# Hybrid attention block on one core: the modulation's vector steps moved to other stages, with their own load queue

## Chip, core and metric

The kernel runs on 1 core of one Trainium2 chip. The metric is device microseconds of one execution. Three runs of the kernel before took 1920.5, 1924.43 and 1924.89 us; their median is 1924.43 us.

The engines are named as in the profile: PE is TensorE (matmul; PEld its weight loads), DVE is VectorE, ACT is ScalarE, POOL is GpSimd and SP is SyncE. SP only issues DMAs here; POOL issues some DMAs and computes a little.

## What is computed

Two layers over 256 latent and 256 context tokens (512 columns in all, kept transposed as `xT`, 1024 features in 8 tiles of 128), in fp32 accuracy.

```python
for layer in range(2):
    mod_x = (silu(c) @ ada_w[layer] + ada_b[layer])        # 9 rows of 1024: shift, scale, gate x 3
    mod_c = (silu(c_ctx) @ ada_w[layer] + ada_b[layer])
    x   = ffn_branch(x, mod_x, 0, ...)     # h + 0.5*gate * swiglu(rms(h)*(1+scale) + shift), d_ff 2816
    ctx = ffn_branch(ctx, mod_c, 0, ...)
    x, ctx = mixer(...)                    # neighbourhood attention, spatial gating, retention; gate row 5
    x   = ffn_branch(x, mod_x, 6, ...)
    ctx = ffn_branch(ctx, mod_c, 6, ...)   # not in the last layer
return x
```

The modulation is a product of a vector with a 1024 x 9216 matrix per layer, once for the latent and once for the context stream ("two streams"). Of layer 1, context needs rows 0 to 4 only.

## The kernel before

**Products.** Each fp32 weight chunk `wr` [128 x up to 1024] is split into a rounded part `wh` (ACT, L89) and the rest `wl` (DVE, L100), and a product is three matmuls (L206 to L208). `Stream` (L64) walks one list of all weight chunks: SP loads into 3 raw buffers, and 4 buffers each hold `wh` and `wl`. `take()` keeps the splits up to three chunks ahead, so the split of an output's next weights stands, on ACT and DVE, ahead of this output's own end.

**FFN.** `ffn(l, f)` runs in two halves of 11 hidden tiles j: up products `g` and `u`, the gate, and then the down products `d` of 8 outputs m with 11 tiles each (`down`, 33 matmuls). After each m DVE adds the result to `xT` (`residual`, L441); in the second half ACT then squares `xT` and DVE sums the squares (`acc`, L341) for the next norm. The last two m of a second half are done one stream at a time (half width), and the statistics (`ss`, L350 on PE, `pow` on POOL at L355) of the latent stream follow while PE does the context's.

FFNs (0, 1) and (1, 0), "direct" in `DIRECT`, do 4 tiles j of the first half plainly and the other 18 by a Winograd scheme (`Seven`) with seven products instead of eight. It needs sums of the normed input, `th` and `tl` [128, 4, 4, 256] each (`sums`: DVE adds, ACT rounds to `th`, DVE subtracts to `tl`), and combined weights `q` and `r`, made by accumulating DMAs from POOL (L529, L530) and a POOL add (L558). After the last tile j of the second half `th` and `tl` are not read again. FFN (1, 1), "one", has the latent stream only.

**Modulation steps.** All of it but two rows of layer 0 is done by DVE: a block `aw` (128 outputs x 1024 inputs, 512 KB) is loaded, and a step (L290, `tensor_tensor_reduce` with the broadcast vector `cb`) gives the 128 values for one stream; a block serves one or two steps. After 8 blocks `fin` adds the bias (L295) and makes the factors (L299, L303). `ada_steps(l, count)` makes the list of these steps for the next blocks of layer l; in front of each step it issues the load of the block that is as many blocks ahead as there are buffers.

**Order.** Code order is engine order (`manual_schedule`). Every product calls `pump`, which adds `pace[0]` (times the product's width over 512) to a credit and takes one item of the list `bg` for each whole credit. So steps stand between products at an even pace, on DVE's one queue, and their loads on SP's one queue, among the weights' loads. A step whose block has not landed holds up all that stands behind it on DVE, and a load whose buffer is not free all that stands behind it on SP.

Before, the 112 steps of layer 1 are divided so: 26 beside FFN (0, 0) after layer 0's 112 (pace 0.34, 5 buffers), 18 beside the first half's and 25 beside the second half's down products of FFNs (0, 1) and (1, 0) each, with 2 buffers that the Winograd `q` shares (tag "aw").

Of the kernel before, what the change touches and what calls it, by code (L numbers as in the profile page):

```python
# [9 lines left out]
F32 = mybir.dt.float32  # L10
F32R = mybir.dt.float32r
# [26 lines left out]

DIRECT = {(0, 1): (4, 0), (1, 0): (4, 0)}

ADA_DOWN = {(0, 1): (18, 25), (1, 0): (18, 25)}

STAT, OS, FS, SPR = 3, 3.5, 2, 12

# [9 lines left out]
SUMS = 1.0  # L54
GPACE = (0.4, 0.55)
OPACE = (0.8, 0.8)
APACE = 0.34
NPACE = (0.95, 1.0)
RPACE = (1.2, 1.4)

# [74 lines left out]
def tile_hybrid_dit(ctx: ExitStack, tc: tile.TileContext, t_x, t_c, t_cb, t_ada0, t_ada, t_adab, t_nw, t_w1, t_w2,  # L135
# [83 lines left out]
    with tc.manual_schedule():  # L219
# [36 lines left out]
        mod = [const.tile([128, 72, 2], F32, name=f"mod{l}") for l in range(L)]  # L256
        amul = [const.tile([128, 3, KT, 2], F32, name=f"amul{l}") for l in range(L)]

        adap = [None, 0]
        cb = const.tile([128, 2, D], F32, name="cb")  # L260

        ada_todo = [[(r, b) for r in range(2 if l == 0 else 0, 9) for b in range(KT)] for l in range(L)]
# [1 line left out]
        def ada_steps(l, count):  # L264

            def streams(r):

                return 1 if l == L - 1 and r > 4 else 2  # L270

            todo = []
            while ada_todo[l] and sum(streams(r) for r, b in todo) < count:
                todo.append(ada_todo[l].pop(0))
            tiles = {}
            nload = [0]

            def loads(n):
                while nload[0] < min(n, len(todo)):
                    r, b = todo[nload[0]]  # L280
                    t = tiles[r, b] = adap[0].tile([128, CHUNK], F32, tag="aw", name="aw", bufs=adap[1])
                    SP.dma_start(out=t, in_=t_ada[l, r, b])
                    nload[0] += 1

            def step(i, s, n):
                loads(i + adap[1])
                r, b = todo[i]
                t = tiles[r, b]
                junk = adap[0].tile([128, CHUNK], F32, tag="cu", name="junk", bufs=1) if s < n - 1 else t
                V.tensor_tensor_reduce(out=junk, in0=t, in1=cb[:, s], scale=1.0, scalar=0.0, op0=ALU.mult, op1=ALU.add,  # L290
                                       accum_out=mod[l][:, 8 * r + b, s:s + 1])

            def fin(r, n):
                mo = mod[l][:, 8 * r:8 * r + 8, 0:n]
                V.tensor_tensor(out=mo, in0=mo, in1=adab[:, l, 8 * r:8 * r + 8].unsqueeze(2).to_broadcast([128, KT, n]),  # L295
                                op=ALU.add)
                i, k = divmod(r, 3)
                if k == 1:
                    V.scalar_tensor_tensor(out=amul[l][:, i, :, 0:n], in0=mo, scalar=1.0,  # L299
                                           in1=nw[:, l, i, :].unsqueeze(2).to_broadcast([128, KT, n]),  # L300
                                           op0=ALU.add, op1=ALU.mult)
                elif k == 2 and i != 1:
                    V.tensor_scalar(out=mo, in0=mo, scalar1=0.5, scalar2=None, op0=ALU.mult)  # L303

            out = [lambda: loads(adap[1])]
            for i, (r, b) in enumerate(todo):
                n = streams(r)
                out += [lambda i=i, s=s, n=n: step(i, s, n) for s in range(n)]
                if b == KT - 1:
                    out.append(lambda r=r, n=n: fin(r, n))  # L310
            return out
# [148 lines left out]
        class Seven:  # L460
# [7 lines left out]

            def __init__(self, pool, gated, l, f):
                self.pool, self.gated, self.l, self.f = pool, gated, l, f  # L470
                self.th = pool.tile([128, 4, 4, T], F32R, name="th")
                self.tl = pool.tile([128, 4, 4, T], F32R, name="tl")
                self.raw, self.part = {}, {}

            def sums(self, q):

                x = []

                def work():
                    t = self.pool.tile([128, CHUNK], F32, tag="cu", name="sum", bufs=1)  # L480
                    u = self.pool.tile([128, NT], F32, tag="ur", name="sum", bufs=1)
                    x.extend(v.rearrange("p (k t) -> p k t", k=2) for v in (t[:, 0:NT], t[:, NT:2 * NT], u))

                a, b = slice(0, T), slice(T, NT)
                k0, k1 = slice(2 * q, 2 * q + 2), slice(4 + 2 * q, 6 + 2 * q)

                def whole(n, k, c):
                    V.tensor_tensor(out=x[n], in0=hTh[:, k, c].bitcast(F32), in1=hTl[:, k, c].bitcast(F32), op=ALU.add)

                def high(i, n, sign=1.0):  # L490
                    S.activation(out=self.th[:, i, k0], in_=x[n], func=AF.Copy, scale=sign)

                def low(i, n, sign=1.0):
                    V.scalar_tensor_tensor(out=self.tl[:, i, k0], in0=x[n], scalar=sign,
                                           in1=self.th[:, i, k0].bitcast(F32), op0=ALU.mult, op1=ALU.subtract)

                def comb(n, p, r, op):
                    V.tensor_tensor(out=x[n], in0=x[p], in1=x[r], op=op)

                def normed(f):  # L500
                    f.when = lambda: all(kt in feeds[self.l, 2 * self.f, n].done for kt in range(KT) for n in range(2))
                    return f

                sub = ALU.subtract
                return [normed(lambda: (work(), whole(0, k0, b))), lambda: whole(1, k0, a),
                        lambda: (comb(1, 1, 0, sub), high(0, 1)), lambda: whole(2, k1, b),
                        lambda: low(0, 1), lambda: (comb(0, 2, 0, sub), high(2, 0)),
                        lambda: (comb(2, 2, 1, ALU.add), high(1, 2, -1.0)), lambda: low(2, 0),
                        lambda: whole(0, k1, a), lambda: low(1, 2, -1.0),
                        lambda: (comb(0, 2, 0, sub), high(3, 0)), lambda: low(3, 0)]  # L510

            def load(self, j):
                if j >= 2 * JH:
# [112 lines left out]
        def ffn(l, f, lead, norms, steps=None, tail=None):  # L626
# [7 lines left out]
            with ExitStack() as es:  # L634
# [8 lines left out]
                def seven_pool():  # L643
                    nonlocal seven
                    pool = es.enter_context(tc.tile_pool(name="seven", bufs=1))
                    seven = Seven(pool, fp, l, f)
                    adap[:] = pool, 2

                if (l, f) in DIRECT:
                    seven_pool()  # L650
                elif not one:
                    adap[:] = fp, ADA_BUFS
                for half in range(2):
                    aTh = fp.tile([128, JH, NT], F32R, tag="aTh", name="aTh")
                    aTl = fp.tile([128, JH, NT], F32R, tag="aTl", name="aTl")
# [116 lines left out]
                                    kt == 0, kt == JH - 1)  # L772

                    split_tail = half == 1 and len(streams) == 2
                    if seven:
                        bg.extend(ada_steps(1, ADA_DOWN[l, f][half]))
                        pace[0], pace[1] = len(bg) / (JH * (KT - 1 if half else KT - 3)), 0.0
                    ahead = seven and half == 0
                    for m in range(KT - 2 if split_tail else KT):
                        a, b = 0, T * len(streams)  # L780
                        wa, wb = ws.take(), ws.take(AHEAD - 1)
                        ps = mm_bank("d")
                        if ahead and m == KT - 3:
                            drain_bg()
                            seven.load(JH)
                            seven.load(JH + 1)
                            seven.add(JH)
# [905 lines left out]
        for l in range(L):  # L1693
# [2 lines left out]
            n2 = {s: Norm(l, 2, s) for s in range(1 if last else 2)}  # L1696
            n3 = {} if last else {s: Norm(l + 1, 0, s) for s in range(2)}
            if l == 0:
                bg.extend(ada_steps(0, 112) + ada_steps(1, 26))
                bg.insert(1, small_inputs)  # L1700
                bg.insert(2, lambda: S.activation(out=cb, in_=cb, func=AF.Silu))
                bg.insert(15, prepare)
# [127 lines left out]
```

## Time and profile before

| | us |
|---|---|
| median of the runs | 1924.43 |
| the profiled execution's own time | 1931.78 |
| its span, first to last instruction | 1929.6 |
| PE busy | 1825.9 (95%) |
| DVE busy | 1312.8 (68%) |
| ACT busy | 728.7 (38%) |
| POOL busy | 239.7 (12%) |
| mean granted TensorE clock, share of full | 0.973 |
| time DMA queues' packets took: SP's, POOL's (share of 16 engines) | 42.7%, 6.5% |

Matmuls are pipelined: a busy PE is one with no gap, and one matmul of 512 columns is listed with some 0.39 us while the next starts 0.23 us after it. Idle time is put down to what ended it. The clock column of a window is the mean over it, 1.00 being full speed.

### The profile page before, as it was taken

The numbers are of one execution on the slowest core, as the hardware profiler recorded it, in microseconds if no ns is written. First come the engines' busy times: TensorE is split into PE (matmuls) and PEld (weight loads), VectorE is DVE, ScalarE is ACT, GpSimd is POOL, SyncE is SP. The second block draws the span as 40 slices with busy tenths as digits, with TensorE's granted clock in tenths as the row PEclk, the third lists the DMA queues.
The fourth block names the chain that finished last, engine by engine and source line by source line (L and its number), as shares of the span: only waits on it lengthen the run. The fifth ranks groups of instructions, "written<-read, shape, count | busy, mean of one in ns | idle before, by whom it ended". The sixth has DMA issues, their size and how long they took to land. (4 is left out here: it accounts for less than half of the span.)

```text
span 1929.6 us, 29556 instructions
## 1 busy us (share of the span) xinstructions
PE 1825.9 (95%) x11592; PEld 1579.8 (82%) x11592; DVE 1312.8 (68%) x2214; ACT 728.7 (38%) x1211; POOL 239.7 (12%) x261
## 2 busy tenths in 40 slices
PE   7999999999999999999999799979987699999999
PEld 5788888887678898978996689869975576889999
DVE  5789888764445567866886678747865554566665
ACT  3322222244542344522452244314421255444443
POOL 0000000011133201202220013002300012410000
PEclk9999999999998999999999899989997799999999
DMA  7756665333111125646754446466745442335555
GB/s 286 244 194 221 227 221 196 123 124 113 61 55 45 55 88 131 147 159 192 188 139 152 135 120 170 141 200 173 170 150 174 139 142 72 99 121 171 180 186 153
DMA packets 104763, 292.19 MB, mean 151 GB/s; under 512 B 12208, under 2 KB 18992, under 8 KB 104496
## 3 DMA queue, kind: packets, MB, share of 16 engines
q1 hardware_dynamic: 94256, 271.43, 42.7%
q0 software_dynamic: 10368, 18.88, 6.5%
q8 instruction: 91, 1.49, 0.3%
q14 instruction: 48, 0.39, 0.1%
HBM read 289.21 MB, written 1.05 MB: 150 GB/s over the span
## 5 line engine op out<-in xcount | busy, mean ns | idle before, releaser
L100 DVE TENSOR_TENSOR wl<-wr,wh 128x1024 fp32r<-128x1024 f32 (+2 forms) x304 | 322.1, 1086 | 109.4 <-ACT wh L89 108.6
L89 ACT CAST wh<-wr 128x1024 fp32r<-128x1024 f32 (+2 forms) x304 | 275.6, 932 | 207.4 <-DMA wr<-in_w_dram 97.8
L206 PE MATMUL d<-aTh,wh 128*128 128x512 f32 (+1 forms) x770 | 281.8, 366 | 43.1 <-ACT wh L89 43.1
L208 PE MATMUL d<-aTh,wl 128*128 128x512 f32 (+1 forms) x770 | 281.1, 365 | 20.1 <-DVE wl L100 20.0
L207 PE MATMUL d<-aTl,wh 128*128 128x512 f32 (+1 forms) x770 | 279.1, 362 | 0.2 <-DVE aTl L680 0.2
L206 PEld LDWEIGHTS d<-aTh,wh 128*128 128x128 f32 x770 | 154.3, 200 | 68.0 <-ACT wh L89 46.9
L290 DVE CUSTOM_DVE_ANT_0 aw<-aw,cb 128x1024 f32<-128x1024 f32 x128 | 156.6, 1223 | 65.4 <-DMA aw<-in_ada_dram 62.5
L208 PEld LDWEIGHTS d<-aTh,wl 128*128 128x128 f32 x770 | 153.5, 199 | 49.1 <-DVE wl L100 27.5
L207 PEld LDWEIGHTS d<-aTl,wh 128*128 128x128 f32 x770 | 153.9, 200 | 22.2 <-DVE aTl L680 0.5
L206 PE MATMUL g<-hTh,wh 128*128 128x512 f32 (+2 forms) x448 | 152.9, 341 | 4.4 <-ACT wh L89 3.4
L207 PE MATMUL g<-hTl,wh 128*128 128x512 f32 (+2 forms) x448 | 151.5, 338 | 1.3 <-DVE hTl L366 1.1
L208 PE MATMUL g<-hTh,wl 128*128 128x512 f32 (+2 forms) x448 | 151.5, 338 | 0.6 <-DVE wl L100 0.5
L208 PE MATMUL u<-hTh,wl 128*128 128x512 f32 (+2 forms) x448 | 150.6, 336 | 0.5 <-DVE wl L100 0.5
L206 PE MATMUL u<-hTh,wh 128*128 128x512 f32 (+2 forms) x448 | 150.3, 336 | 0.0
L207 PE MATMUL u<-hTl,wh 128*128 128x512 f32 (+2 forms) x448 | 150.3, 335 | 0.0
L290 DVE CUSTOM_DVE_ANT_0 junk<-aw,cb 128x1024 f32<-128x1024 f32 x96 | 117.1, 1220 | 41.1 <-DMA aw<-in_ada_dram 40.6
L214 PE MATMUL nat<-wh,hTh 128*128 128x512 f32 (+2 forms) x384 | 138.3, 360 | 0.0
L216 PE MATMUL nat<-wh,hTl 128*128 128x512 f32 (+2 forms) x384 | 128.5, 335 | 0.4 <-DVE hTl L366 0.4
L215 PE MATMUL nat<-wl,hTh 128*128 128x512 f32 (+2 forms) x384 | 128.4, 334 | 0.0
L583 PE MATMUL p<-hTh,wl 128*128 128x256 f32 x432 | 124.1, 287 | 1.6 <-DVE wl L552 0.5
L583 PE MATMUL p<-th,wl 128*128 128x256 f32 x432 | 122.0, 282 | 0.2 <-DVE wl L552 0.2
L582 PE MATMUL p<-hTl,wh 128*128 128x256 f32 x432 | 121.4, 281 | 0.0
(261 smaller groups left out, 4106.6 us busy)
## 6 DMA issues: line engine op xcount, KB each, us to landing
aw<-in_ada_dram SPq DMA_DIRECT2D x144, 512.0 KB, 5.0
wr<-in_w_dram SPq DMA_DIRECT2D x140, 512.0 KB, 4.4
wr<-in_wi_dram SPq DMA_DIRECT2D x56, 512.0 KB, 3.6
wr<-in_w_dram SPq DMA_DIRECT2D x64, 384.0 KB, 3.6
wr<-in_w_dram SPq DMA_DIRECT2D x64, 320.0 KB, 2.9
q<-in_w_dram SPq DMA_DIRECT2D x72, 256.0 KB, 3.3
q<-in_w_dram POOLq DMA_DIRECT2D x72, 256.0 KB, 5.6
ur<-in_w_dram SPq DMA_DIRECT2D x36, 256.0 KB, 4.4
```

What stands on the lines that cost most here:

```text
L89: self.nc.scalar.copy(out=h[:, :n], in_=self.raw[i][:, :n])
L100: self.nc.vector.tensor_tensor(out=lo[:, :n], in0=t[:, :n], in1=h[:, :n].bitcast(F32), op=ALU.subtract)
L206: PE.matmul(out=ps, lhsT=wh[:, col:col + 128], rhs=hh[rhs_sl], start=start, stop=False)
L207: PE.matmul(out=ps, lhsT=wh[:, col:col + 128], rhs=hl[rhs_sl], start=False, stop=False)
L208: PE.matmul(out=ps, lhsT=wl[:, col:col + 128], rhs=hh[rhs_sl], start=False, stop=stop)
L214: PE.matmul(out=ps, lhsT=hh[lhs_sl], rhs=wh[:, wc], start=start, stop=False)
L215: PE.matmul(out=ps, lhsT=hh[lhs_sl], rhs=wl[:, wc], start=False, stop=False)
L216: PE.matmul(out=ps, lhsT=hl[lhs_sl], rhs=wh[:, wc], start=False, stop=stop)
L290: V.tensor_tensor_reduce(out=junk, in0=t, in1=cb[:, s], scale=1.0, scalar=0.0, op0=ALU.mult, op1=ALU.add, accum_out=mod[l][:, 8 * r + b, s ...
L582: PE.matmul(out=ps, lhsT=wh[:, cw], rhs=tl, start=False, stop=False)
L583: PE.matmul(out=ps, lhsT=wl[:, cw], rhs=th, start=False, stop=n == 3)
```

## The change

Four things change. The steps of layer 1 are divided anew (`ADA1`): 48 beside FFN (0, 0) at pace 0.355, none beside the first halves of (0, 1) and (1, 0), 27 and 29 beside their second halves' down products, 8 beside the up products of the last FFN's first half. The lists take whole blocks, so 28, 29 and 7 steps stand there; they need 14, 27 and 7 loads. In the second halves the four buffers are quarters of a tile with the tag of `th`, so they lie in its memory, and the loads are issued by POOL. In FFN (1, 1) there are four buffers of its own pool, loaded by SP. In `sums` each cast to `th` stands one item later than the sum that it reads (13 items instead of 12).

```diff
-ADA_DOWN = {(0, 1): (18, 25), (1, 0): (18, 25)}
+ADA1 = {(0, 0): 48, (0, 1): 27, (1, 0): 29, (1, 1): 8}
...
-APACE = 0.34
+APACE = 0.355
...
-        adap = [None, 0]
+        adap = [None, 0, SP, None]
...
                     r, b = todo[nload[0]]
-                    t = tiles[r, b] = adap[0].tile([128, CHUNK], F32, tag="aw", name="aw", bufs=adap[1])
-                    SP.dma_start(out=t, in_=t_ada[l, r, b])
+                    t = tiles[r, b] = adap[0](nload[0])
+                    adap[2].dma_start(out=t, in_=t_ada[l, r, b])
...
-                junk = adap[0].tile([128, CHUNK], F32, tag="cu", name="junk", bufs=1) if s < n - 1 else t
+                junk = adap[3].tile([128, CHUNK], F32, tag="cu", name="junk", bufs=1) if s < n - 1 else t
...
-                self.th = pool.tile([128, 4, 4, T], F32R, name="th")
+                self.th = pool.tile([128, 4, 4, T], F32R, tag="th", name="th")
...
-                return [normed(lambda: (work(), whole(0, k0, b))), lambda: whole(1, k0, a),
-                        lambda: (comb(1, 1, 0, sub), high(0, 1)), lambda: whole(2, k1, b),
-                        lambda: low(0, 1), lambda: (comb(0, 2, 0, sub), high(2, 0)),
...
+                return [normed(lambda: (work(), whole(0, k0, b))), lambda: whole(1, k0, a), lambda: comb(1, 1, 0, sub),
+                        lambda: (whole(2, k1, b), high(0, 1)), lambda: comb(0, 2, 0, sub),
+                        lambda: (low(0, 1), high(2, 0)), lambda: comb(2, 2, 1, ALU.add),
...
                     seven = Seven(pool, fp, l, f)
-                    adap[:] = pool, 2
 
                 if (l, f) in DIRECT:
                     seven_pool()
-                elif not one:
-                    adap[:] = fp, ADA_BUFS
+                else:
+                    nb = ADA_BUFS - one
+                    adap[:] = lambda i: fp.tile([128, CHUNK], F32, tag="aw", name="aw", bufs=nb), nb, SP, fp
+                if one:
+                    bg.extend(ada_steps(1, ADA1[l, f]))
+                    pace[0], pace[1] = len(bg) / (KT * (JH - 1)), 0.0
...
-                    if seven:
-                        bg.extend(ada_steps(1, ADA_DOWN[l, f][half]))
-                        pace[0], pace[1] = len(bg) / (JH * (KT - 1 if half else KT - 3)), 0.0
+                    if one and half == 0:
+                        drain_bg()
+                    if seven and half:
+
+                        aw = seven.pool.tile([128, 4, CHUNK], F32, tag="th", name="aw")
+                        adap[:] = lambda i: aw[:, i % 4], 4, G, seven.pool
+                        bg.extend(ada_steps(1, ADA1[l, f]))
+                        pace[0], pace[1] = len(bg) / (JH * (KT - 1)), 0.0
...
                         if ahead and m == KT - 3:
-                            drain_bg()
                             seven.load(JH)
...
-                bg.extend(ada_steps(0, 112) + ada_steps(1, 26))
+                bg.extend(ada_steps(0, 112) + ada_steps(1, ADA1[0, 0]))
```

How instructions move is seen at three places. The first is DVE at the end of the second half of FFN (0, 0); `d` are the down products, `ss` the statistics of the next norm. Before, from the residual of the last full-width output m = 5 on (the sums of squares, L341, are left out in both):

```order
L441 SCALAR_TENSOR_TENSOR xT_69<-d_3011,mod0_93,xT_69 128x256 x2
L100 TENSOR_TENSOR wl_3055<-wr_2955,wh_3053 128x768
L100 TENSOR_TENSOR wl_3061<-wr_3003,wh_3059 128x640
L441 SCALAR_TENSOR_TENSOR xT_69<-d_3065,mod0_93,xT_69 128x256
L441 SCALAR_TENSOR_TENSOR xT_69<-d_3103,mod0_93,xT_69 128x256
L353 TENSOR_SCALAR v_3158<-ss_3153 128x2
```

Now, from the same residual on (each step's row that reads the accumulator is left out):

```order
L441 SCALAR_TENSOR_TENSOR xT_69<-d_3056,mod0_93,xT_69 128x256 x2
L100 TENSOR_TENSOR wl_3106<-wr_2990,wh_3104 128x768
L100 TENSOR_TENSOR wl_3112<-wr_3048,wh_3110 128x640
L290 ISA junk_3132,mod1_94<-aw_2999,cb_97 128x1024
L290 ISA aw_2999,mod1_94<-aw_2999,cb_97 128x1024
L441 SCALAR_TENSOR_TENSOR xT_69<-d_3116,mod0_93,xT_69 128x256
L290 ISA junk_3173,mod1_94<-aw_3022,cb_97 128x1024
L290 ISA aw_3022,mod1_94<-aw_3022,cb_97 128x1024
L441 SCALAR_TENSOR_TENSOR xT_69<-d_3157,mod0_93,xT_69 128x256
L295 TENSOR_TENSOR mod1_94<-mod1_94,adab_78 128x16
L303 TENSOR_SCALAR mod1_94<-mod1_94 128x16
L353 TENSOR_SCALAR v_3217<-ss_3212 128x2
```

The steps (L290) used to end with the third output; now they go on to the last half-width residual, and `fin` (L295, L303) stands directly in front of the statistics' `v`.

The second place is the queue that issues the blocks `aw` in the second half's down products of FFN (1, 0). Before, it is SP's, and `wr` are the weights of the down products:

```order
L79 DMA wr_13155<-in_w2_dram 128x640 [waits DMAHW1_49,DVE_49]
L79 DMA wr_13161<-in_w2_dram 128x768 [waits DMAHW4_49,DMAHW2_49,DVE_49]
L282 DMA aw_13167<-in_ada_dram 128x1024 [waits DMAHW3_49]
L282 DMA aw_13176<-in_ada_dram 128x1024 [waits DVE_49]
L282 DMA aw_13188<-in_ada_dram 128x1024 [waits DMAHW5_49,DVE_49]
L282 DMA aw_13200<-in_ada_dram 128x1024 [waits DMAHW6_49,DVE_49]
L79 DMA wr_13221<-in_w2_dram 128x640 [waits DMAHW7_49,DVE_49]
L79 DMA wr_13227<-in_w2_dram 128x768 [waits DMAHW1_49,DMAHW0_49,DVE_49]
```

Now it is POOL's, behind the last POOL add of the Winograd weights:

```order
L557 TENSOR_TENSOR wr_12523<-wr_12523,q_12525 128x512 [waits DMASW4_49,DMAHW7_49,DVE_49,Activation_49]
L282 DMA aw_12917<-in_ada_dram 128x1024 [waits PE_49]
L282 DMA aw_12917<-in_ada_dram 128x1024 x3
L282 DMA aw_12917<-in_ada_dram 128x1024 [waits DVE_49]
L282 DMA aw_12917<-in_ada_dram 128x1024 [waits DMASW3_49,DVE_49]
L282 DMA aw_12917<-in_ada_dram 128x1024 [waits DVE_49]
L282 DMA aw_12917<-in_ada_dram 128x1024 [waits DMASW5_49,DVE_49]
```

The loads left SP's queue, where four of them stood between two pairs of weights; on POOL nothing but loads follows until the statistics. The first waits for PE, the last reader of `th`.

The third place is DVE at the start of the second half's down products of FFN (0, 1) now, with the semaphores that each step waits for (accumulator rows left out); `aw` is the one tile with four quarters:

```order
L290 ISA junk_9221,mod1_94<-aw_9191,cb_97 128x1024 [waits DMASW4_49]
L290 ISA aw_9191,mod1_94<-aw_9191,cb_97 128x1024 [waits DVE_49]
L290 ISA junk_9240,mod1_94<-aw_9191,cb_97 128x1024 [waits DMASW5_49]
L441 SCALAR_TENSOR_TENSOR xT_69<-d_9198,mod0_93,xT_69 128x256 [waits PE_49]
L441 SCALAR_TENSOR_TENSOR xT_69<-d_9198,mod0_93,xT_69 128x256
L100 TENSOR_TENSOR wl_9250<-wr_9138,wh_9248 128x768 [waits DMAHW0_49,Activation_49]
L100 TENSOR_TENSOR wl_9256<-wr_9172,wh_9254 128x640 [waits DMAHW1_49,Activation_49]
L290 ISA aw_9191,mod1_94<-aw_9191,cb_97 128x1024 [waits DVE_49]
L290 ISA junk_9278,mod1_94<-aw_9191,cb_97 128x1024 [waits DMASW6_49]
L290 ISA aw_9191,mod1_94<-aw_9191,cb_97 128x1024 [waits DVE_49]
L290 ISA junk_9297,mod1_94<-aw_9191,cb_97 128x1024 [waits DMASW7_49]
```

The first step on each block waits for the next DMA semaphore of POOL's queue in turn (DMASW4, 5, 6, 7), the second step on a block for none.

## Rows read from the trace of the kernel before

**Rows 1.** Windows, down-product stages: span, busy us (instructions) by engine, PEclk, DMA share, GB/s.

```profile
160.40:222.00 61.60, 61.60 (x266) 49.48 (x265) 56.44 (x95) 14.51 (x19) 0.00 (x0) 1.00 0.71 238
344.40:407.40 63.00, 63.00 (x342) 53.83 (x342) 39.20 (x70) 19.02 (x34) 0.69 (x1) 1.00 0.31 99
830.90:899.70 68.80, 64.01 (x267) 50.49 (x266) 41.60 (x69) 13.23 (x18) 4.86 (x5) 0.98 0.62 189
1011.90:1102.60 90.70, 74.72 (x344) 61.74 (x342) 59.53 (x106) 19.11 (x35) 0.72 (x1) 0.87 0.43 142
1224.70:1305.30 80.60, 66.76 (x267) 51.98 (x266) 42.81 (x71) 13.83 (x18) 4.81 (x5) 0.94 0.61 192
1415.80:1532.50 116.70, 78.48 (x343) 64.49 (x342) 57.66 (x104) 19.11 (x35) 0.71 (x1) 0.80 0.48 159
```

**Rows 2.** Waits, 1415.8 to 1532.5: who waited for whom, us, times, longest.

```profile
DVE aw L290 <- DMA aw<-in_ada_dram: 46.7, 12, 6.2
...
PE d L206 <- ACT wh L89: 31.2, 5, 9.7
```

**Rows 3.** Waits, 1224.7 to 1305.3.

```profile
PE d L208 <- DVE wl L100: 13.6, 4, 5.5
```

**Rows 4.** Waits of SP's queue, 1415.8 to 1532.5.

```profile
SPq L282 <- DVE mod L290: 40.5, 15, 7.0
```

**Rows 5.** Timeline of DVE from 1458.5: start, us, operation [idle before <- releaser].

```profile
1458.51 0.87 DVE L441 SCALAR_TENSOR_TENSOR xT<-d,mod,xT 128x256 f32<-128x256 f32 x2
1459.47 0.82 DVE L341 TENSOR_TENSOR acc<-acc,sq 128x256 f32<-128x256 f32 x2
1460.58 1.70 DVE L100 TENSOR_TENSOR wl<-wr,wh 128x768 fp32r<-128x768 f32 x2 [0.30 <-ACT wh L89]
1462.19 1.22 DVE L290 CUSTOM_DVE_ANT_0 aw<-aw,cb 128x1024 f32<-128x1024 f32 x1
...
1468.94 1.23 DVE L290 CUSTOM_DVE_ANT_0 aw<-aw,cb 128x1024 f32<-128x1024 f32 x1 [5.52 <-DMA aw<-in_ada_dram]
...
1473.89 1.23 DVE L290 CUSTOM_DVE_ANT_0 aw<-aw,cb 128x1024 f32<-128x1024 f32 x1 [2.46 <-DMA aw<-in_ada_dram]
...
1475.04 0.87 DVE L441 SCALAR_TENSOR_TENSOR xT<-d,mod,xT 128x256 f32<-128x256 f32 x2
```

**Rows 6.** Timeline of DVE, first step of FFN (0, 1)'s second half.

```profile
1021.68 1.23 DVE L290 CUSTOM_DVE_ANT_0 junk<-aw,cb 128x1024 f32<-128x1024 f32 x1 [4.45 <-DMA aw<-in_ada_dram]
```

**Rows 7.** Timeline, statistics at the end of FFN (0, 1).

```profile
1093.52 0.38 PE L350 MATMUL ss<-ones,sq 128*128 128x1 f32 x2 [3.21 <-ACT sq L337]
```

**Rows 8.** Windows, first 50 us.

```profile
0.00:50.00 50.00, 37.36 (x328) 28.02 (x329) 26.01 (x66) 17.42 (x35) 1.60 (x6) 1.00 0.80 291
```

**Rows 9.** Timeline of POOL, an accumulating DMA's issue.

```profile
785.71 1.19 POOL L530 DMA_DIRECT2D q<-in_w_dram  x1
```

**Rows 10.** Waits of DVE, 60 to 345 (first FFN).

```profile
DVE sg L673 <- PE u L208: 5.6, 7, 1.4
...
DVE xT L441 <- PE d L208: 4.1, 5, 1.5
```

**Rows 11.** Windows, up products of the last FFN's first half.

```profile
1740.00:1805.00 65.00, 65.00 (x541) 65.00 (x540) 43.75 (x68) 32.48 (x47) 0.00 (x0) 1.00 0.50 163
```

**Rows 12.** Waits, 725 to 760 (the sums of FFN (0, 1)).

```profile
ACT th L491 <- DVE sum L498: 14.6, 6, 3.3
...
PE g L206 <- ACT wh L89: 2.3, 1, 2.3
```

**Rows 13.** The page's part 6: DMA issues, count, KB each, us to landing.

```profile
aw<-in_ada_dram SPq DMA_DIRECT2D x144, 512.0 KB, 5.0
...
q<-in_w_dram SPq DMA_DIRECT2D x72, 256.0 KB, 3.3
q<-in_w_dram POOLq DMA_DIRECT2D x72, 256.0 KB, 5.6
```

**Rows 14.** Windows, 750 to 800 (Winograd products).

```profile
750.00:800.00 50.00, 49.95 (x379) 47.80 (x378) 38.98 (x51) 25.04 (x38) 14.96 (x14) 1.00 0.71 175
```

More of the change, by code (lines that the diff above doesn't have):

```diff
@@ L504, in sums @@
                 sub = ALU.subtract
-                return [normed(lambda: (work(), whole(0, k0, b))), lambda: whole(1, k0, a),
-                        lambda: (comb(1, 1, 0, sub), high(0, 1)), lambda: whole(2, k1, b),
-                        lambda: low(0, 1), lambda: (comb(0, 2, 0, sub), high(2, 0)),
-                        lambda: (comb(2, 2, 1, ALU.add), high(1, 2, -1.0)), lambda: low(2, 0),
-                        lambda: whole(0, k1, a), lambda: low(1, 2, -1.0),
-                        lambda: (comb(0, 2, 0, sub), high(3, 0)), lambda: low(3, 0)]
+                return [normed(lambda: (work(), whole(0, k0, b))), lambda: whole(1, k0, a), lambda: comb(1, 1, 0, sub),
+                        lambda: (whole(2, k1, b), high(0, 1)), lambda: comb(0, 2, 0, sub),
+                        lambda: (low(0, 1), high(2, 0)), lambda: comb(2, 2, 1, ALU.add),
+                        lambda: (low(2, 0), high(1, 2, -1.0)), lambda: whole(0, k1, a), lambda: low(1, 2, -1.0),
+                        lambda: comb(0, 2, 0, sub), lambda: high(3, 0), lambda: low(3, 0)]
             def load(self, j):
```

## Prediction

> **What bounds the kernel now.** I first read the busy shares and the clock in the table above: TensorE is busy for 95% of the span and DVE for 68%, so only time in which TensorE waits, or runs below its full clock, can be won. Next I cut the span into the stages of the code. The down products of the first three FFNs have the same shape, 8 outputs m of 11 x 3 matmuls, so the stage without a wait is a ruler: 61.6 us for a first half and 63.0 us for a second half [rows 1]. The reader is to see in the other four windows that the same products take 68.8, 90.7, 80.6 and 116.7 us, with DMA at half its share and the granted clock at 0.80 to 0.98. The excess is 7.2 + 27.7 + 19.0 + 53.7 = 107.6 us: nearly all that TensorE loses in this kernel, and all of it beside the modulation steps with two buffers.
>
> Then the waits. In the worst window DVE stands 46.7 us before steps whose block `aw` has not landed, and TensorE stands 31.2 us for `wh` [rows 2]; in the first half of FFN (1, 0) it stands 13.6 us for `wl` [rows 3]. The queue of SP shows the loop: it stands 40.5 us before an `aw` load until a step frees one of the two buffers, and the weights' loads stand behind it [rows 4]. One turn of DVE closes it [rows 5]: residuals, sums of squares, the two splits of the next weights, a step, then 5.52 us for a load, two steps, 2.46 us for the next. In order, the residual and the splits wait behind the late block; the turn takes 16.5 us where TensorE needs 61.6 / 8 = 7.7. The clock's part (0.80 over the worst window, so some of it at 1.2 instead of 2.4 GHz) goes with the gaps: 78.48 us busy there against 63.00 for the same matmuls [rows 1].
>
> **The change part by part.** (1) *First halves of (0, 1) and (1, 0): no steps.* 18 steps and 9 or 13 loads leave each. What stays is the ruler's work without its steps. Excess 7.2 + 19.0 = 26.2; what could be late next is the combined weights for the Winograd products, whose DMAs now start earlier, so I leave 1.2. **-25.0** (bounds -26.2 and -20).
>
> (2) *Second half of (0, 1): 28 steps instead of 26, 14 loads on POOL's queue, four buffers.* Two blocks are needed per m, so four buffers cover a load of 5 us, and the waits for blocks go. DVE is late next. By rows 5 the fixed part of a turn is 1458.51 to 1462.19 = 3.7 us, and four steps of about 1.2 us are 4.8: 8.5 against 7.7, a lag of 0.8 per m. The first load cannot start before the last product with `th`, and DVE waited 4.45 us for it even on SP [rows 6]; I take 2.4 us of lag for that. At m = 5 the lag is 2.4 + 5 x 0.8 - 1.2 (one m has three steps) + 0.6 (fins and one m with five) = 5.8. A lag stops TensorE only beyond 7.7 - 2.9 = 4.8 (the splits follow the residual by 2.9): 1 us. In the tail a half-width m takes 3.9 us, so the last weights are 5.8 + 2.9 - 3.9 = 4.8 us late, and the statistics' matmul `ss` waits for the last square as it does now, 3.21 us [rows 7], about 3.7 with three steps in front of it. 63.0 + 1 + 4.8 + 3.7 + 1 for the clock = 73.5. **-17** (bounds -27.7 and -8).
>
> (3) *Second half of (1, 0): 29 steps but 27 loads*, since most blocks now serve one stream. DVE alone would give 73.5 + 1.5 = 75. The loads weigh more: an m needs 0.72 MB of weights and 4.3 blocks of 0.524 MB, 2.97 MB. The best long window, the first 50 us, moves 291 GB/s at a share of 0.80 [rows 8]: 10.2 us per m at that rate, 8.2 at 291 / 0.80. I take 9.9, 1.4 over DVE's turn, for six m's, and 1.6 for the first loads: 85. **-31.7**. Bounds: 66 us if all is hidden (-50.7), and 116.7 if nothing changes (0). The order rows of the change (second pair) show that the loads no longer stand among SP's weights. POOL's 27 issues of up to 1.2 us [rows 9] delay nobody: only the statistics' `pow` stands behind them, four blocks later.
>
> (4) *First FFN: 22 more steps, up to its end.* 22 x 1.22 = 27 us of DVE. From 60 to 345 us DVE has waited for TensorE for 4.1 + 5.6 = 9.7 us [rows 10], which is what the higher pace (0.355 for 0.34) adds there, about 9 steps of 1.2. The other 13 steps stand beside the second half's down products, where DVE used to be free (39.2 us of 63 [rows 1]). With steps a turn is 8.5 for 7.7; by the count of (2), starting from 0.5 lag, 3.8 at m = 5: no stop before the tail, then 3.8 + 2.9 - 3.9 = 2.8 for weights and 2.5 for `ss`, and 1.7 for the ups. **+7** (bounds 0 and +27, no cover at all).
>
> (5) *Last FFN: 7 steps, 4 + 3 loads on SP.* DVE is 43.8 of 65 us busy there [rows 11], which hides 8.5 us of steps. The first four loads go out together: 2.1 MB, about 6 to 7 us of DMA time before the next weights, against a stream that is one pair of weights ahead. **+2** (0 to +8.5).
>
> (6) *Sums' casts lag.* ACT now asks for a sum one product after DVE makes it. ACT stood 14.6 us for these sums in the first of its two stretches, but TensorE only 2.3 us, once, for a weight cast [rows 12]. **0** (-2 to +2).
>
> Sum: -25.0 - 17 - 31.7 + 7 + 2 = -64.7. The profiled execution took 1931.8 us, 2.2 outside its span; that gives 1867. It lies 7.4 above the median of the runs, 1924.4; for that median, **1860 us**.
>
> **Rivals.** *A, the loads stay the bound (0.15).* A load of 256 KB lands 5.6 us after issue from POOL's queue and 3.3 from SP's; blocks on SP take 5.0 [rows 13]. If landing doubles with four in flight beside the weights (11), four blocks take 11 + 1.2 issue + 1.2 step = 13.4 us, 27 of them 90, and with the tail the window is 105; (0, 1) only starts later, 78. -25 - 12.7 - 11.7 + 9 = -40: 1884. For it: demand of 2.97 MB per m is near the best rate seen. Against: 24 loads in 117 us are far from that rate now, because the two-buffer loop spaces them.
>
> *B, DVE's lag costs nothing (0.15).* If the statistics and splits fit the slack, the second halves take 66 us each, the first FFN pays 1: -26 - 24.7 - 50.7 + 1 = -100: 1824. For it: the ruler's tail hides everything; against: DVE has no step beside the ruler's last three m's, and now has some there (first pair of order rows).
>
> *C, slower: POOL's loads starve (0.04).* DVE runs 57 steps with two SBUF operands back to back while POOL has to issue loads. The 41 loads run in rounds of four, 10.25 rounds; every microsecond that landing grows beyond 8 costs 10 us, so from 14.3 us of landing the gain of 64.7 is gone, and at 20 us the kernel would take 1983. Against: where POOL's loads run now, DVE is 78% busy (38.98 of 50 us), and they land at 5.6 us [rows 13, 14]. The Trainium skill (SBUF — State Buffer, SBUF: two separate sides) warns of just this: a DVE operation in a two-port mode locks GpSimd out, the descriptors are not written, and a transfer of 620 ns becomes 3100 ns; it advises the SP or ACT queue. The trace rather disagrees for the operations seen here, as 5.6 us shows; no row shows it beside steps. By the page, 2.5 us more per round, the estimate would be 1860 + 10.25 x 2.5 = 1886, about rival A.
>
> *D, the four quarters act as one buffer (0.02).* Then each of the 41 steps' blocks would be waited for in full, some 8 us: about 200 us slower. The last order rows speak against it: the steps wait for different DMA semaphores in turn.
>
> **How the numbers follow.** The forecast has 0.64. Its own range: (3) alone spans 76 to 98, (2) 66 to 80, (4) 0 to 14, together about 1843 to 1877. To hold 8 in 10 I reach to A and towards B: 1828 to 1890. A difference under 0.3% (6 us) cannot be told from no change. Forecast, A and B are faster: 0.93 with something taken off for what I have not seen; C and D slower with the same remainder: 0.05; 0.02 between.
>
> **What would show it.** Right: the windows of first halves at 62 with no `aw` wait; the second halves of (0, 1) and (1, 0) at 73 and 85 with a clock near 1; TensorE waiting there for `wl`, `wh` and `ss` behind DVE, not DVE for `aw` (in (1, 0) some 5 to 15 us of it); a few us of new waits at the end of the first FFN. Wrong: `aw` waits of over 30 us in (1, 0) (A, or with landing above 14 us C), a first FFN longer by 15 us or more, or no new wait in any tail (B).

## The result and the profile after

The changed kernel takes 1842.66 us (median of 4 runs, 1841.88 to 1846.93) against 1923.74 before: a ratio of 0.9586, interval 0.9567 to 0.9605. The forecast was 1860 us, with a range of 1828 to 1890; the kernel became faster by 81 us instead of 64. The page's first part, and from the waits of TensorE the two groups for weights of down products:

```profile
span 1840.1 us, 29560 instructions
PE 1791.2 (97%) x11592; PEld 1556.0 (85%) x11592; DVE 1310.0 (71%) x2214; ACT 729.4 (40%) x1211; POOL 262.2 (14%) x302
```

```profile
PE d L206 <- ACT wh L89: 12.1, 3, 6.6
...
PE d L208 <- DVE wl L100: 1.9, 6, 0.5
```

The columns of the second view are us in all, times and the longest: 14 us now, against 43.1 and 20.0 in the same two groups before. The same stages as in [rows 1], in the same columns:

```profile
157.10:219.20 62.10, 61.87 (x265) 49.26 (x264) 60.26 (x102) 14.45 (x18) 0.00 (x0) 1.00 0.75 243
341.80:412.30 70.50, 66.58 (x342) 56.98 (x341) 59.44 (x107) 19.01 (x34) 0.70 (x1) 0.95 0.46 150
828.50:890.00 61.50, 61.50 (x266) 49.43 (x265) 24.13 (x35) 14.60 (x19) 4.87 (x5) 1.00 0.48 142
1000.60:1071.40 70.80, 66.63 (x345) 56.96 (x344) 61.13 (x108) 19.19 (x35) 8.33 (x15) 0.95 0.57 189
1192.20:1253.70 61.50, 61.50 (x266) 49.43 (x265) 22.88 (x35) 14.40 (x19) 4.90 (x5) 1.00 0.46 140
1364.30:1439.60 75.30, 67.30 (x344) 55.84 (x343) 62.37 (x115) 19.11 (x35) 15.09 (x28) 0.95 0.78 268
```

The two first halves of (0, 1) and (1, 0) run in 61.5 us, the ruler's time (61.6). The second halves fell from 90.7 and 116.7 to 70.8 and 75.3; in return the first FFN's second half rose from 63.0 to 70.5. These six differences sum to -79.7 us, so the stages named in the prediction hold nearly all of the gain. The profiled execution fell by more, 89.5 us. Of the rest, 7.3 us lie between the first FFN and FFN (0, 1), where TensorE's clock in the execution before fell after work that the changed kernel runs through at full clock; first before, then after:

```profile
600.00:625.00 25.00, 24.33 (x147) 21.53 (x147) 12.31 (x26) 5.04 (x10) 8.91 (x6) 0.82 0.13 43
```

```profile
605.00:630.00 25.00, 24.35 (x180) 22.11 (x178) 13.79 (x29) 5.04 (x10) 8.89 (x6) 1.00 0.12 43
```

Another 3.3 us lie ahead of the first down products. Both look like scatter between executions and not like the change: in the profiles of the changed kernel and of all experiments the first of these stages takes 416.2 to 417.8 us (423.5 before, in its one profile), and the first down products start at 156.9 to 160.7 us even within the changed kernel's own profiles. The execution before lay 7.4 us above its median.

What is left in the second half of (1, 0), on DVE from the last full-width residual but one, and then on TensorE:

```profile
1410.16 0.87 DVE L441 SCALAR_TENSOR_TENSOR xT<-d,mod,xT 128x256 f32<-128x256 f32 x2
...
1412.30 1.69 DVE L100 TENSOR_TENSOR wl<-wr,wh 128x768 fp32r<-128x768 f32 x2 [0.30 <-ACT wh L89]
1413.91 1.22 DVE L290 CUSTOM_DVE_ANT_0 aw<-aw,cb 128x1024 f32<-128x1024 f32 x1
...
1420.47 1.23 DVE L290 CUSTOM_DVE_ANT_0 aw<-aw,cb 128x1024 f32<-128x1024 f32 x1 [1.90 <-DMA aw<-in_ada_dram]
...
1421.62 0.87 DVE L441 SCALAR_TENSOR_TENSOR xT<-d,mod,xT 128x256 f32<-128x256 f32 x2
```

```profile
1416.92 0.28 PE L208 MATMUL d<-aTh,wl 128*128 128x256 f32 x1
1423.78 0.58 PE L206 MATMUL d<-aTh,wh 128*128 128x256 f32 x1 [6.59 <-ACT wh L89]
...
1427.93 0.41 PE L207 MATMUL d<-aTl,wh 128*128 128x256 f32 x1
1428.14 0.41 PE L208 MATMUL d<-aTh,wl 128*128 128x256 f32 x1
...
1429.49 0.28 PE L206 MATMUL d<-aTh,wh 128*128 128x256 f32 x1
1429.61 0.28 PE L207 MATMUL d<-aTl,wh 128*128 128x256 f32 x1
```

Between the splits of one pair of weights (the row of 1412.30 holds both) and the residual of the last full-width output, at 1421.62, stand five steps and a wait of 1.90 us for a block. The weights of the next output are cast behind that residual; by then TensorE has finished a half-width output and stands for 6.59 us. After that wait the matmuls start every 0.21 us instead of every 0.12; the window of that stretch shows the clock at half, the level of 1.2 GHz:

```profile
1423.80:1429.30 5.50, 5.30 (x23) 5.00 (x24) 4.96 (x9) 0.97 (x2) 0.00 (x0) 0.50 0.82 273
```

From 1423.78 to 1429.49 start 24 matmuls in 5.7 us, 0.2 of it a wait for `wl`. At the 0.117 us from start to start of the output before they would take 2.8, so the slow stretch behind the gap costs some 2.7 us more.

### The profile page after: what moved, and what is told of

Same layout as the page of the kernel before. It is cut to its first block, busy times and chain, and to the rows that moved or that the text cites. A ratio compares the mean times of both kernels' runs of the same rounds, so it can differ in the third digit from the quotient of the medians.

```text
span 1840.1 us, 29560 instructions
## 1 busy us (share of the span) xinstructions
PE 1791.2 (97%) x11592; PEld 1556.0 (85%) x11592; DVE 1310.0 (71%) x2214; ACT 729.4 (40%) x1211; POOL 262.2 (14%) x302
## 5 line engine op out<-in xcount | busy, mean ns | idle before, releaser
L206 PE MATMUL d<-aTh,wh 128*128 128x512 f32 (+1 forms) x770 | 273.5, 355 | 12.3 <-ACT wh L89 12.1
L208 PE MATMUL d<-aTh,wl 128*128 128x512 f32 (+1 forms) x770 | 272.8, 354 | 1.9 <-DVE wl L100 1.9
L207 PE MATMUL d<-aTl,wh 128*128 128x512 f32 (+1 forms) x770 | 271.9, 353 | 0.2 <-DVE aTl L682 0.2
L206 PEld LDWEIGHTS d<-aTh,wh 128*128 128x128 f32 x770 | 148.4, 193 | 35.3 <-ACT wh L89 14.1
L208 PEld LDWEIGHTS d<-aTh,wl 128*128 128x128 f32 x770 | 148.0, 192 | 24.9 <-DVE wl L100 4.0
L207 PEld LDWEIGHTS d<-aTl,wh 128*128 128x128 f32 x770 | 148.4, 193 | 21.5 <-DVE aTl L682 0.5
L290 DVE CUSTOM_DVE_ANT_0 aw<-aw,cb 128x1024 f32<-128x1024 f32 x128 | 155.4, 1223 | 7.4 <-DMA aw<-in_ada_dram 4.9
L581 PE MATMUL p<-hTl,wh 128*128 128x256 f32 x432 | 121.4, 281 | 0.0
L580 PE MATMUL p<-hTh,wh 128*128 128x256 f32 x432 | 121.1, 280 | 0.0
```

What stands on the lines that cost most here:

```text
L206: PE.matmul(out=ps, lhsT=wh[:, col:col + 128], rhs=hh[rhs_sl], start=start, stop=False)
L207: PE.matmul(out=ps, lhsT=wh[:, col:col + 128], rhs=hl[rhs_sl], start=False, stop=False)
L208: PE.matmul(out=ps, lhsT=wl[:, col:col + 128], rhs=hh[rhs_sl], start=False, stop=stop)
L580: PE.matmul(out=ps, lhsT=wh[:, cw], rhs=th, start=n == 0, stop=False)
L581: PE.matmul(out=ps, lhsT=wh[:, cw], rhs=tl, start=False, stop=False)
```

## Experiments

**Queue and buffers, three kernels.** The changed kernel with the queue, the buffers or both undone in the second halves; each line stands in place of the first (the comments name the kernels):

```diff
-aw[:, i % 4], 4, G, seven.pool
+aw[:, i % 4], 4, SP, seven.pool      # e1_sp_queue
+aw[:, i % 2], 2, G, seven.pool       # e2_two_buffers
+aw[:, i % 2], 2, SP, seven.pool      # e3_sp_two
```

> The changed kernel with one thing undone: in the second halves of FFNs (0, 1) and (1, 0) the blocks are loaded by SP again, among the weights, but into four buffers. Theory (the number of buffers is what removed the waits; the queue adds little): with three blocks ahead SP seldom stands before a load, the windows of the two second halves stay near the 70.7 and 75.1 us of the changed kernel, at most 5 us longer each, 1843 to 1853 us in all. Rival (the queue is what mattered, since the weights stood behind late blocks): TensorE waits for wh again, both windows grow by 10 to 25 us, 1865 to 1890 us.

> The changed kernel with two quarters of the tile in use instead of four, still loaded by POOL. Theory (buffers): two blocks turn in one landing (5.3 us) plus an issue (1.2) plus a step (1.2), 3.85 us a block; the 27 loads of (1, 0) then take 104 us and its window grows by about 25 to 30 us with waits of DVE for aw; the 14 loads of (0, 1) take 54 us, so its window grows by 0 to 5. 1868 to 1878 us. Rival (the queue was all): DVE waits, but the weights no longer stand behind the blocks and the windows grow by under 5 us each: 1843 to 1853.

> The changed kernel with both undone: two buffers, loaded by SP, but with the new division of the steps. Theory (loop of two buffers with the weights behind the blocks, as in the kernel before, where 24 loads took 116.7 us): 27 loads take 120 to 130 us in the second half of (1, 0), 14 loads about 85 to 91 in that of (0, 1): 1905 to 1920 us, so that only the first halves' 26 us are kept, less what the first FFN pays. Rival (the division of the steps did most of it): the windows stay under 80 and 95, below 1875 us.

Measured, with the interval of the ratio to before: 1865.11 us (0.967 to 0.9708), 1882.73 (0.9766 to 0.9795) and 1910.38 (0.9912 to 0.9941). The second halves of (0, 1) and (1, 0) in the three, in that order:

```profile
1003.60:1080.50 76.90, 68.64 (x344) 56.51 (x343) 61.78 (x108) 19.11 (x35) 0.72 (x1) 0.96 0.53 173
...
1372.80:1462.80 90.00, 71.57 (x343) 58.29 (x342) 62.94 (x115) 19.15 (x35) 0.71 (x1) 0.91 0.66 225
```

```profile
1002.60:1086.00 83.40, 70.24 (x345) 58.81 (x344) 62.08 (x108) 19.12 (x35) 8.32 (x15) 0.92 0.49 160
...
1378.50:1478.90 100.40, 72.96 (x344) 60.15 (x343) 63.37 (x115) 19.11 (x35) 15.04 (x28) 0.85 0.62 201
```

```profile
1002.70:1093.00 90.30, 71.92 (x345) 58.81 (x344) 62.19 (x108) 19.17 (x35) 0.72 (x1) 0.91 0.46 148
...
1385.60:1506.60 121.00, 78.81 (x343) 64.44 (x343) 63.77 (x115) 19.07 (x35) 0.71 (x1) 0.80 0.51 166
```

Against the changed kernel (1842.66) the buffers are worth 40 us, the queue 22, both 68: nearly a plain sum. The changed kernel itself gave 1842.66 to 1847.30 in three sets of runs, so each is good to some 5 us; the two windows alone give 38, 21 and 65. With both undone the new division of the steps (and the lag of the casts) is what is left; it is worth 14 us of the 81, a difference under 2%. The theory "buffers alone" fell for the first kernel: 1843 to 1853 was expected and the lower edge of its rival, 1865, came, though with windows that grew by 6.1 and 14.7 us where the rival had 10 to 25 for each. For the second, (0, 1) grew by 12.6 us instead of 0 to 5 and (1, 0) by 25.1 as expected, so that the total passed the expected 1878 by 5. For the third the theory held. Waits of SP's queue in the second half of (1, 0), of the first kernel and then of the kernel before:

```profile
SPq L79 <- DVE wl L100: 50.1, 14, 12.7
SPq L282 <- DVE mod L290: 21.8, 17, 4.6
```

```profile
SPq L79 <- DVE wl L100: 54.3, 15, 15.2
```

The prediction read only the line of `mod` ([rows 4], 40.5 us before): weights behind late blocks. The line of `wl` is the other half, and before the change it was the longer one: blocks behind weights, whose loads wait until DVE has split the weights that hold the buffer.

**Loads and steps apart.** One kernel issues only the first four loads of each second half, so that its later steps read what those left; the other leaves the first FFN's 22 added steps out, and with them the blocks at the end of the list. Both compute something else than the reference, and each ran once.

```diff
-                    adap[2].dma_start(out=t, in_=t_ada[l, r, b])
+                    if adap[2] is SP or nload[0] < 4:                   # e5_few_loads
+                        adap[2].dma_start(out=t, in_=t_ada[l, r, b])
```

```diff
-ADA1 = {(0, 0): 48, (0, 1): 27, (1, 0): 29, (1, 1): 8}
+ADA1 = {(0, 0): 26, (0, 1): 27, (1, 0): 29, (1, 1): 8}                 # e6_first26
...
-APACE = 0.355
+APACE = 0.34
...
```

> The changed kernel, in which each of the two second halves issues only its first four block loads; the later steps read what those left behind, so the modulation is not the reference's. DVE's steps are all there. Theory (the lag of DVE behind TensorE sets both windows, the loads cost only the two waits of 3.9 us for a block in (1, 0)): the window of (0, 1) stays at 70 to 71 us, that of (1, 0) falls from 75.3 to 71 to 72. Rival (the traffic of the loads, 268 GB/s, slows the weights and the steps too): both fall below 68 us.

> The changed kernel with 26 steps beside FFN (0, 0) at pace 0.34, as before the change; the 22 steps that this pushes out at the end of the list are left out altogether, so parts of the modulation are zero. Two things are read. First FFN: theory (the 13 steps beside the second half's down products make DVE late in the tail; the ups have cover): its second window falls from 70.5 to 63 us, the first from 62.1 to 61.6, the start of the down products stays within 1 us. Rival (the higher pace costs the up products too): the first window starts 3 us or more earlier as well. FFN (1, 0): its 29 steps now need 16 loads instead of 27; theory: the window falls by the waits for blocks, from 75.3 to 71 to 72 us. Rival (loads never mattered there, the steps alone): 75.

The second halves of (0, 1) and (1, 0) without the later loads:

```profile
1003.10:1073.80 70.70, 65.20 (x344) 55.62 (x343) 61.05 (x108) 19.15 (x35) 2.94 (x5) 0.98 0.33 115
1366.80:1437.80 71.00, 65.78 (x344) 55.93 (x343) 62.23 (x115) 19.17 (x35) 2.90 (x5) 0.95 0.33 114
```

In (0, 1) the loads cost nothing that one profile can show (70.8 with them, 72.2 and 73.8 in two more profiles of the changed kernel); in (1, 0) they cost 4.3, or 3 to 5 with the scatter of its profiles. What stays is DVE's lag, as the theory had it. The total is no shorter (1842.7): its first down products start 2.5 us later than the changed kernel's, and the stage before the last FFN's down products took 273.8 us instead of 271.1. The latter goes with the clock, 0.83 from 1595 to 1615 us, where the changed kernel shows 1.00 (1580 to 1640). The former is a slow start, read further down. In the second kernel (1834.28, one run):

```profile
157.50:219.00 61.50, 61.50 (x265) 49.43 (x264) 56.46 (x95) 14.44 (x18) 0.00 (x0) 1.00 0.72 235
341.60:404.50 62.90, 62.90 (x342) 53.80 (x341) 39.18 (x70) 19.02 (x34) 0.70 (x1) 1.00 0.30 99
```

The first FFN pays 0.6 + 7.6 us for its 22 steps, all in the down products, which start at the same time as the changed kernel's (157.5 and 157.1). The window of (1, 0) with 16 loads is 74.2: no wait for a block is left there, yet TensorE still stands 4.8 us for `wh`. This is nearer to the rival's 75 than to the 71 to 72 of the theory; but five profiles of the changed kernel's tail (with the old sums or not) lie between 74.1 and 75.9, so one profile can't say more.

**The lag of the casts.** `sums` with the 12 items of before, in two sets of runs, the second beside the changed kernel:

```diff
-lambda: comb(1, 1, 0, sub), lambda: (whole(2, k1, b), high(0, 1)), ...
+lambda: (comb(1, 1, 0, sub), high(0, 1)), lambda: whole(2, k1, b), ...
```

> The changed kernel with the old list of the sums (each cast to th beside the sum that it reads, 12 items). Theory: no difference that can be measured, 1841 to 1845 us, since ACT's waits for sums do not reach TensorE. Rival: the 1 to 2 us by which the stages between the down products became shorter (112.2 to 110.4 and 122.1 to 120.9 us) come from the lag; then 1845 to 1848.

> The changed kernel itself, once more and beside the others, so that the small difference to the kernel with the old list of sums (1847.8 us) is read from more runs. If the lag of the casts is worth something, 1841 to 1845 us; if that difference was between chips or runs, 1846 to 1850.

> Once more the changed kernel with the old list of the sums, beside the changed kernel on the same chip, in more rounds. Before: 1847.8 us against 1842.7 and 1843.4. Theory: under 2 us apart, 1842 to 1846. Rival: the lag of the casts is worth 4 to 5 us: 1846 to 1849 with no overlap of the runs.

> The changed kernel, as the partner of the run before: 1841 to 1845 us under either theory.

1847.76 us against 1843.38 for the changed kernel looked like 4 us; side by side on one chip they are 1848.25 (0.9579 to 0.9615) and 1847.30 (0.9582 to 0.9608): no difference that totals can tell. The partner itself missed its expected 1841 to 1845, so most of the 4 us lay between sets of runs. The profiles show where. The first down products of the changed kernel start at 156.9 us in the first of its two sets here and at 160.7 in the second. One matmul ahead of them, in that order:

```profile
27.45 0.40 PE L207 MATMUL u<-hTl,wh 128*128 128x512 f32 x1
```

```profile
29.67 0.63 PE L207 MATMUL u<-hTl,wh 128*128 128x512 f32 x1
```

Matmuls of 512 columns took 0.63 us up to 32.5 us in the second of these profiles and 0.40 from 21 us on in the first; in the kernel that issues only four loads they took 0.63 up to 30.0, in the changed kernel's first profile up to 25.7. What the lag of the casts itself gives shows in single stages: that from the first FFN to FFN (0, 1) takes 417.2 us in both profiles with the old sums and 416.2 in all three of the changed kernel, the next one from (0, 1) to (1, 0) 121.4 and 121.8 against 120.1 to 120.9, some 1 us each.

**Steps back into the first halves.** A try at a faster version, then the same with other numbers, then with POOL's queue in the first halves:

```diff
-ADA1 = {(0, 0): 48, (0, 1): 27, (1, 0): 29, (1, 1): 8}
+ADA1 = {(0, 0): 38, (0, 1): (14, 20), (1, 0): (14, 22), (1, 1): 4}   # e7_spread
+ADA1 = {(0, 0): 42, (0, 1): (16, 22), (1, 0): (8, 20), (1, 1): 4}    # e9_spread2, e10_spread2_pool
...
+adap[:] = lambda i: sp.tile([128, CHUNK], F32, tag="aw", name="aw", bufs=2), 2, SP, sp   # first halves, e7 and e9
+adap[:] = lambda i: sp.tile([128, CHUNK], F32, tag="aw", name="aw", bufs=2), 2, G, sp    # first halves, e10
...
```

In the second and third the steps of the second halves also end one output earlier. These two kernels differ in one word, the queue.

> A try at a faster version: 38 steps beside FFN (0, 0), 14 and 20 beside the two halves of (0, 1), 14 and 22 beside those of (1, 0), 4 beside the last FFN; in the first halves two buffers of their own loaded by SP, as before the change, in the second halves four quarters loaded by POOL. Theory (what is left is the lag of DVE, so about three steps per output fit without any): (0, 0) second window 63 to 65, the second halves of (0, 1) and (1, 0) 64 to 67 each, the first halves 62 to 64: about 1822 us. Rival (two buffers on SP hold the weights again in the first halves, as the 18 steps did for 7.2 and 19.0 us): the first halves at 68 to 75, 1832 to 1845 us.

> The first try at spreading (1831.0 us) with other numbers: 42 steps beside FFN (0, 0), 16 and 22 beside the halves of (0, 1), 8 and 20 beside those of (1, 0), 4 beside the last FFN; in the second halves the pace ends the steps with the last full-width output. Theory: in the first half of (1, 0) each step on a single-stream block needs a load of its own, and two buffers of SP's queue were late for 14 of them (19 us of DVE waits, window 69.9); 8 fit, so that window falls to 63 or 64; in the second half no step stands beside the tail, so its window falls from 68.4 to 64 to 66; (0, 0) stays at 63 to 65. About 1824 us. Rival: 42 steps in the first FFN are already late in its tail and 22 in (0, 1) too, which eats the gain: 1829 to 1834.

> The same spread as the run before, but the loads of the first halves come from POOL's queue instead of SP's. Theory: with few steps the queue hardly matters; SP stood before such loads for 2.3 and 9.9 us with 14 steps, so at most 2 us less: 1822 to 1825. Rival: POOL issues there the accumulating loads and the adds for the next Winograd weights, and blocks in front of them make those late: 1826 to 1832.

Totals: 1830.97 us (0.9482 to 0.9529), 1834.24 (0.9515 to 0.9544) and **1823.21** (0.9456 to 0.9484). The first and second miss the expected 1822 and 1824. The windows of the first came out as expected or shorter but for those of (1, 0), 69.9 and 68.4 us: in its first half the rival held. In the second, the second half of (0, 1) with its 22 steps took 67.9, as its rival feared. The last has the expected total and beats the changed kernel of the same set (1847.30) by 24 us, but not for the expected reason: it was to gain 2 us at most on a kernel of 1824, and gained 11 on one of 1834, so that the total is luck. The first halves of (0, 1) and (1, 0) with SP's queue, then with POOL's:

```profile
824.20:891.50 67.30, 64.48 (x266) 51.30 (x265) 39.43 (x65) 13.43 (x18) 4.85 (x5) 0.95 0.60 186
...
1192.20:1260.60 68.40, 63.84 (x266) 50.35 (x265) 31.51 (x52) 13.88 (x18) 4.82 (x5) 0.98 0.61 188
```

```profile
825.30:886.80 61.50, 61.50 (x266) 49.44 (x265) 43.47 (x69) 14.37 (x19) 8.06 (x11) 1.00 0.64 192
...
1185.80:1247.30 61.50, 61.50 (x266) 49.44 (x266) 32.32 (x52) 14.75 (x19) 8.01 (x11) 1.00 0.63 190
```

With 8 steps in place of 14 the first half of (1, 0) on SP's queue did not get the 63 or 64 us that were expected, and that the queue hardly matters with few steps was wrong. The timelines show why. SP's queue in the first half of (1, 0) with SP's loads, one turn of DVE, and a wait of SP's queue over this window:

```profile
1207.09 1.06 SPq L79 DMA_DIRECT2D wr<-in_w_dram  x2
1208.20 1.09 SPq L282 DMA_DIRECT2D aw<-in_ada_dram  x2
1217.25 1.06 SPq L79 DMA_DIRECT2D wr<-in_w_dram  x2
```

```profile
1206.12 1.68 DVE L100 TENSOR_TENSOR wl<-wr,wh 128x768 fp32r<-128x768 f32 x2
1207.72 1.22 DVE L290 CUSTOM_DVE_ANT_0 aw<-aw,cb 128x1024 f32<-128x1024 f32 x1
...
1214.33 1.23 DVE L290 CUSTOM_DVE_ANT_0 aw<-aw,cb 128x1024 f32<-128x1024 f32 x1 [5.39 <-DMA aw<-in_ada_dram]
...
1216.27 1.68 DVE L100 TENSOR_TENSOR wl<-wr,wh 128x768 fp32r<-128x768 f32 x2
```

```profile
SPq L79 <- DVE wl L100: 39.4, 11, 8.2
```

The block is issued only after the weights, these only after DVE's splits, and the next splits only after the step on the block: a turn of 10.2 us where TensorE needs 7.7, with just two steps in it. On POOL's queue the loads leave when a buffer is free, and the loop is gone. The second half of (1, 0) in the kernel with SP's first halves shows the rest:

```profile
1371.20:1434.00 62.80, 62.80 (x343) 53.73 (x342) 51.42 (x93) 19.14 (x35) 11.34 (x21) 1.00 0.75 263
```

With 20 steps that end before the tail it takes the ruler's time, while its loads and weights move 263 GB/s, nearly as much as the 268 of the changed kernel: the traffic by itself costs TensorE nothing there.

## Why the prediction was right, and where its sizes were off

Three readings in the prediction were off without changing its course. The excess of 107.6 us is not nearly all that TensorE loses: 31 of its 104 us of idle time lie outside the four windows. Of the 22 added steps of the first FFN, 17 stand beside the second half's down products (27 instead of 10), not 13. And 27 blocks over seven outputs are 3.9 per output, not 4.3.

(1) *First halves.* Forecast -25.0; -26.4 by the windows (7.3 + 19.1). Right, but the reason was incomplete: on POOL's queue, with 16 and 8 steps where 18 each stood before, the same windows are 61.5 too. It was the loads' place in SP's queue that cost the time, and not the steps; for (1, 0) this is shown for 8 steps only.

(2) *Second half of (0, 1).* Forecast 73.5; 70.8, and 72.2 and 73.8 in two more profiles of the same kernel. The turn is as worked out: from residual to residual 8.47 us (five turns from 1009.47 to 1051.80), 8.5 in the prediction. Its other terms were mis-sized, and the errors partly cancel. The first load cost nothing, where 2.4 us of lag were taken: DVE was still busy with the gate and a split when the block landed, and the first step started without a wait. The stop of 1 us before the tail did not come. In the tail TensorE waited 3.1 to 3.5 us for weights and 0.9 to 1.9 for the statistics, instead of 4.8 and 3.7. The half-speed stretch took 3.6 (66.63 us busy for 63.00) instead of 1.

(3) *Second half of (1, 0).* Forecast 85; 75.3 (74.1 to 75.9 in three profiles). This is most of the miss, by one term: "I take 9.9, 1.4 over DVE's turn, for six m's, and 1.6 for the first loads", 10 us for the loads; the kernel without them puts it at 4.3. The 9.9 came from the best rate before, 291 GB/s at a share of 0.80 [rows 8], and from 4.3 blocks per output. The first 50 us of this window move more, while TensorE is 98% busy; below it is DVE's wait for blocks over the whole window:

```profile
1364.30:1414.30 50.00, 48.79 (x210) 37.86 (x209) 43.74 (x79) 12.89 (x24) 11.72 (x22) 1.00 0.89 304
```

```profile
DVE aw L290 <- DMA aw<-in_ada_dram: 3.9, 2, 2.0
```

DVE waits for a block only twice, against 46.7 us [rows 2], both times in a turn with five steps; four buffers let loads run ahead in the turns with four, and the first loads were early here too. DVE alone gives 71.0, not 75, by the terms of (2).

(4) *First FFN.* Forecast +7; +8.0 by the windows (0.5 and 7.5), and the kernel with 26 steps gives 8.2. The size is right, in part by luck: in the tail TensorE waited 2.4 us for `wh` and 1.0 for `ss` (2.8 and 2.5 forecast), the clock took 3.6 (66.58 us busy for 63.00), which the sum left out, and the 1.7 us taken for the up products did not come.

(5) *Last FFN.* Forecast +2. The stage from (1, 0)'s end to the last down products grew from 267.8 to 271.1 us; TensorE now waits 2.6 us there for `wl` and 0.8 for `wh`. But 4 steps instead of 8 gave 269.5 to 273.0 in three kernels, and in the two that took about 273 the clock was at 0.86 over 25 us there; so it is not resolved better than 1 to 5 us.

(6) *Casts.* Forecast 0 (-2 to +2); no difference in the totals, some 1 us in each of two stages.

The rivals. *A* (1884) expected a landing of 11 us; the 41 blocks on POOL's queue landed after 3.9 to 8.0, median 5.3 (the last row below). *B* (1824) had no tail waits; they are there, 3 and 7 us, though smaller than forecast. *C*: POOL issues a load in 0.53 us in the median, 0.61 at most, while DVE runs steps, and the longest landing is 8.0, far from 14.3:

```profile
aw<-in_ada_dram SPq DMA_DIRECT2D x103, 512.0 KB, 4.9
...
aw<-in_ada_dram POOLq DMA_DIRECT2D x41, 512.0 KB, 5.3
```

```profile
DMA to landing us min/median/max: 3.9/5.3/8.0
```

The Trainium skill (SBUF — State Buffer, SBUF: two separate sides) has DVE in a two-port mode lock GpSimd out of writing descriptors. The trace shows no such delay beside this step, which reads two operands from SBUF in fp32; whether the step runs in such a mode no run here shows. Issuing these loads from SP, as the same section of the Trainium skill advises against that delay, cost 22 us here (1865.11). *D* is out: two quarters in place of four cost 40 us, so the four do not act as one.

## What to carry to other kernels

A load in an in-order queue waits for whatever the loads ahead of it wait for. Where a background load shares a queue with weights that wait for an engine which in turn waits for that load, the loop sets the turn, even with two steps in it. Give such loads another queue, and count their buffers against the turn of the engine that uses them: in the second halves neither did it alone (the queue was worth 22 us, the buffers 40); in the first halves, with few loads, the queue with two buffers was enough. When the waits are gone, see what the moved work does to the tail, where outputs are short: there a late step reaches TensorE at once, and a stretch at the lower clock adds to it.

## What the runs showed of the hardware that was not expected

A wait of 6.6 us on TensorE was followed by 5.5 us at the lower of its two clock levels, which added about 2.7 us. One of 3.1 us, in the second half of (0, 1), was followed by 6.4 us at that level (0.50 from 1054.0 to 1060.4), so that there the slow stretch cost about as much as the wait itself.

A block of 512 KB lands about as fast from POOL's queue as from SP's: in the second half of (1, 0), with 27 loads and four buffers, after 4.6 to 8.0 us, median 5.6, from POOL's (changed kernel) and after 3.9 to 8.0, median 6.6, from SP's (first of the three kernels). POOL's issue of it takes 0.53 us, about half of the 1.19 for an accumulating one [rows 9].

The first matmuls of an execution ran slower for a time that differed between profiles of one kernel: matmuls of 512 columns were listed with 0.63 us up to 25.7 us in one, up to 32.5 in another, and with 0.40 from 21 us on in a third. This moves everything behind them by up to 3.8 us, most of the 4.5 by which the spans of the second and third of these profiles differ.
